# Layer B's q as seven products for eight, with weight operands made in layer A and kept in DRAM

## The chip, the cores and the metric

The kernel runs on one core of one Trainium2 chip. The metric is the time of the kernel on the device in microseconds (us). Before the change the median of three runs is 1050.8 us (1050.23 to 1050.91).

## The reference

The input x is 1024 tokens by 1024 channels in float32. Layer A is a gated MLP on chunks of 128 tokens, layer B is sliding-window attention. Cut to what matters:

```python
# layer A
h = rms_norm(x, a_pre_g)
u, v, z = split(h @ w_in, 3)                 # each 1024 x 2048
v = layer_norm(gelu(v), ln_g, ln_b)          # then in 8 groups of 256 channels
s = causal(w_s[group]) @ v[chunk] + b_s
h = x + rms_norm((gelu(u) * s * silu(z)) @ w_out, a_post_g)
# layer B
k = rms_norm(h, kv_norm_g) @ w_k             # 1024 x 256, 4 heads of 64
v = rms_norm(h, kv_norm_g) @ w_v
q, z = split(rms_norm(h, b_pre_g) @ b_w_in, 2)   # each 1024 x 1024, 16 heads of 64
logits = q k^T / 8 + alibi                   # window of 128 back, with a sink per head
o = softmax(logits with sink) @ v
out = h + rms_norm((o * silu(z)) @ b_w_out, b_post_g)
```

## The kernel before

Each float32 product is made from two float32r parts. A value is split into a high part (a copy on ScalarE) and a low part (the rest, a subtraction on DVE), and `mm3` (L168 to L171) issues three matmuls: high times high, high times low, low times high. One matmul has 128 rows, 128 columns of weights and mostly 512 columns of tokens, half of the sequence. The halves are called h = 0 and 1.

In layer A the three big products (`v_layer`, `uz_layer`, `out_layer`) use a scheme of seven products of half-size matrices instead of eight: the two token halves and the two halves of the inner dimension give sums and differences of the inputs, and the same is done with the weights, on DVE, GpSimd and ScalarE. In layer B all products are plain.

Layer B runs in this order. `q_phase(0)` makes q for the first half (192 matmuls of 512 columns), while `chain_a(1)` finishes layer A's output h1 for the second half beside it. `kv_phase(0)` makes k and v (48 matmuls of 512 columns and 96 of 256). `z_phase(0)` makes the gate z (192). Then `attn(0)` runs the attention of the first half. Attention's matmuls come in small groups with softmax work on DVE, ScalarE and GpSimd between them, so `attn` fills the gaps from a generator: `more` takes a share of 64 fill steps at each of 40 places. The fill of `attn(0)` is `kv_phase(1)`, `q_phase(1)` and the first half of `z_phase(1)`. `attn(1)` is filled with the second half of z and with the output product `out_b`.

The weights of layer B go through the class `Weights` (L112 on). `order` lists the pieces of 512 KB in the order of their use, `load` fetches a raw piece on the queue of SyncE (SP), and `split` makes whi (ScalarE, L109) and wlo (DVE, L110), scaled by the gain of the norm. Three raw buffers and two buffers each of whi and wlo take turns. A weight that is used by both halves is fetched and split twice.

The order of the instructions on each engine is set by a scheduler that goes by the program's order, dependencies and its own estimates. It may move an instruction ahead of another, except where `keep_in_program_order` pins it. Each engine then works through its list in that order, and an instruction that waits holds all behind it. Loads and stores are issued on the queue of SP; a few stores are issued on the queue of ScalarE (ACT); GpSimd (POOL) issues none. A tile whose tag has fewer buffers than tiles waits until the last reader of the old content is done.

At the start of the program GpSimd has a cast, two selects (`affine_select`, L593) that cut the causal triangle of the weights w_s, and then `rx`, the factors of the first norm, for which ScalarE's gelu waits.

## Time and profile before

| what | number |
|---|---|
| median of three runs | 1050.8 us |
| profiled execution | 1051.19 us |
| its span | 1049.4 us |
| TensorE (PE) busy | 1038.2 us, 99% |
| VectorE (DVE) busy | 731.8 us, 70% |
| ScalarE (ACT) busy | 579.8 us, 55% |
| GpSimd (POOL) busy | 199.5 us, 19% |
| granted TensorE clock, mean | 0.998 |
| moved by DMA | 157.56 MB, 150 GB/s over the span |

The span goes from the first to the last instruction of the trace, and the profiled execution's own time is 1.8 us longer. A share of busy time is an average over the span: stages of the program differ, and what a wait costs is read at its own place. "A <- B" in a list of waits says that A stood still until B's result was there.

### The profile page before, as it was taken

Reading aid. Unit: us, or ns where it says so; the run is one execution under the profiler, and the core shown is the slowest. Engines: PE = TensorE matmul, PEld = TensorE weight load, DVE = VectorE, ACT = ScalarE, POOL = GpSimd, SP = SyncE. Lnnn points to the kernel's source line nnn. Section 1 sums busy time; section 2 is a strip of 40 time slices with the busy share of each in tenths; the row PEclk is TensorE's granted clock in tenths of the full one; section 3 lists DMA queues with packets and bytes.
Section 4 is the critical chain, followed back from the end, with each engine's and each line's share of the span. In section 5 each row is a group of like instructions: output and inputs, shape, how many; then the busy total and the mean of one; then the engine's idle time right before and its main releaser. Section 6 shows DMA issues by size and latency. Waiting matters only on the chain.

```text
span 1049.4 us, 13678 instructions
## 1 busy us (share of the span) xinstructions
PE 1038.2 (99%) x4994; PEld 854.8 (81%) x4994; DVE 731.8 (70%) x1244; ACT 579.8 (55%) x998; POOL 199.5 (19%) x153
## 2 busy tenths in 40 slices
PE   9999999999999999999999999999999999999997
PEld 7878888888888888888888888888888777877776
DVE  6987566867768668677696587765247786667763
ACT  6584344565565465655444465654466665786631
POOL 0500003253442552530200000100001111011120
PEclk9999999999999999999999999999999999999999
DMA  8878242324333333247998543532322121211363
GB/s 309 271 262 292 101 171 94 116 101 146 126 117 120 123 134 116 101 140 265 320 354 282 195 167 93 200 102 82 99 81 66 56 81 61 81 61 62 121 220 121
DMA packets 80899, 157.56 MB, mean 150 GB/s; under 512 B 5824, under 2 KB 32704, under 8 KB 80832
## 3 DMA queue, kind: packets, MB, share of 16 engines
q1 hardware_dynamic: 76320, 148.01, 41.4%
q10 hardware_dynamic: 4512, 8.68, 2.3%
q8 instruction: 39, 0.64, 0.3%
q14 instruction: 28, 0.23, 0.1%
HBM read 125.21 MB, written 31.46 MB: 149 GB/s over the span
## 4 chain that ended last, share of the span: by engine, by line
PE 93%; DVE 3%; DMA 2%; ACT 1%; issue 0%; SPq 0%; DVEq 0%; POOLq 0%; ACTq 0%
PE qz L169 6%; PE ob L169 6%; PE ub L169 6%; PE qz L171 6%; PE ub L170 6%; PE ub L171 6%; PE ob L171 6%; PE ob L170 6%; PE qz L170 6%; PE s L1058 3%; PE uc L170 3%; PE uc L169 3%; PE uc L171 3%; PE sp L621 3%; PE oc L169 2%; PE oc L171 2%
## 5 line engine op out<-in xcount | busy, mean ns | idle before, releaser
L110 DVE SCALAR_TENSOR_TENSOR wlo<-raw_w,gn,whi 128x512 fp32r<-128x512 f32 x80 | 58.5, 757 | 62.2 <-ACT whi L109 62.0
L169 PE MATMUL qz<-n_hi,whi 128*128 128x512 f32 x256 | 100.9, 394 | 0.0
L171 PE MATMUL qz<-n_hi,wlo 128*128 128x512 f32 x256 | 99.8, 390 | 1.1 <-DVE wlo L110 1.1
L170 PE MATMUL qz<-n_lo,whi 128*128 128x512 f32 x256 | 99.9, 390 | 0.0
L109 ACT ACTIVATE whi<-raw_w,gn 128x512 fp32r<-128x512 f32 x80 | 54.8, 716 | 56.8 <-PE qz L170 36.6
L1073 ACT ACTIVATE pr<-pr,mx 128x129 f32<-128x129 f32 x128 | 50.1, 393 | 39.8 <-DVE mx L1069 39.8
L169 PEld LDWEIGHTS qz<-n_hi,whi 128*128 128x128 f32 x256 | 48.1, 188 | 15.8 <-issue 5.7
L105 ACT ACTIVATE uzhilo_g<-f 128x1024 fp32r<-128x1024 f32 x31 | 32.9, 1060 | 49.2 <-PE uc L171 43.3
L171 PEld LDWEIGHTS qz<-n_hi,wlo 128*128 128x128 f32 x256 | 48.0, 188 | 11.8 <-DVE wlo L110 1.5
L170 PEld LDWEIGHTS qz<-n_lo,whi 128*128 128x128 f32 x256 | 48.1, 188 | 9.3
L106 DVE TENSOR_TENSOR uzhilo_g<-f,uzhilo_g 128x1024 fp32r<-128x1024 f32 x31 | 38.6, 1245 | 19.9 <-ACT uzhilo_g L105 19.9
L209 ACT ACTIVATE uz_slots<-ub 128x512 f32<-128x512 f32 x48 | 28.3, 590 | 42.4 <-PE ub L171 39.2
L169 PE MATMUL ub<-T,whi_g 128*128 128x512 f32 x128 | 50.7, 396 | 0.0
L169 PE MATMUL ub<-T,uzhilo_g 128*128 128x512 f32 x128 | 50.5, 395 | 0.0
L171 PE MATMUL ub<-T,wlo_g 128*128 128x512 f32 x128 | 49.9, 390 | 0.0
L171 PE MATMUL ub<-T,uzhilo_g 128*128 128x512 f32 x128 | 49.9, 390 | 0.0
L170 PE MATMUL ub<-T,uzhilo_g 128*128 128x512 f32 x128 | 49.9, 390 | 0.0
L170 PE MATMUL ub<-T,whi_g 128*128 128x512 f32 x128 | 49.8, 389 | 0.0
L169 PE MATMUL uc<-T,uzhilo_g 128*128 128x512 f32 x124 | 48.9, 395 | 0.0
L170 PE MATMUL uc<-T,uzhilo_g 128*128 128x512 f32 x124 | 48.3, 389 | 0.0
L171 PE MATMUL uc<-T,uzhilo_g 128*128 128x512 f32 x124 | 48.3, 389 | 0.0
L105 ACT ACTIVATE whi_g<-raw_uz 128x1024 fp32r<-128x1024 f32 (+1 forms) x31 | 26.5, 854 | 36.8 <-PE ua L170 14.3
(334 smaller groups left out, 3078.3 us busy)
## 6 DMA issues: line engine op xcount, KB each, us to landing
raw_uz<-in_wuz_in_dram SPq DMA_DIRECT2D x32, 512.0 KB, 3.4
raw_w<-in_wqz_dram SPq DMA_DIRECT2D x32, 512.0 KB, 3.5
td<-uz_slots SPq DMA_DIRECT2D x56, 256.0 KB, 2.2
orawP2a<-td SPq DMA_DIRECT2D x28, 512.0 KB, 4.1
raw<-in_wv_in_dram SPq DMA_DIRECT2D x17, 512.0 KB, 4.8
vg<-vd SPq DMA_DIRECT2D x8, 1024.0 KB, 5.3
orawP2b<-in_wo_a_dram SPq DMA_DIRECT2D x16, 512.0 KB, 8.2
vraw<-in_wv_in_dram SPq DMA_DIRECT2D x13, 512.0 KB, 4.8
```

The costliest lines, as they stand in the source:

```text
L105: nc.scalar.activation(hi, src, AF.Copy)
L106: nc.vector.tensor_tensor(lo, src, hi.bitcast(F32), ALU.subtract)
L109: nc.scalar.activation(hi, src, AF.Copy, scale=g)
L110: nc.vector.scalar_tensor_tensor(lo, src, g, hi.bitcast(F32), ALU.mult, ALU.subtract)
L169: nc.tensor.matmul(out, lhsT=a_hi, rhs=b_hi, start=start, stop=False, skip_group_check=True)
L170: nc.tensor.matmul(out, lhsT=a_hi, rhs=b_lo, start=False, stop=False, skip_group_check=True)
L171: nc.tensor.matmul(out, lhsT=a_lo, rhs=b_hi, start=False, stop=stop, skip_group_check=True)
L209: nc.scalar.activation(out, a, AF.Copy)
L621: nc.tensor.matmul(psv[:, n], lhsT=d["vg"][:, 4 * j + n, i * P:(i + 1) * P], rhs=d["wc"], start=True, stop=True)
L1058: nc.tensor.matmul(pss[par][:, g, w0:256], lhsT=q[par][:, m, bs_], rhs=w[par][:, p, ks], start=g + k == 0, stop=g + k == 2, skip_group_che ...
L1073: nc.scalar.activation(pr[:, i], pr[:, i], AF.Exp, bias=mx[:, i:i + 1], scale=-1.0, accum_out=dn[:, i:i + 1])
```

## The change

q of both halves becomes seven products for eight. The operands on the side of the tokens are made from n0 and n1, the normed inputs of both halves, in `norm_sums`: T1 and T2 are the two inner halves of n0, T3 is one of n1, and T4 to T7 are sums, split anew. The operands on the side of the weights are made in layer A: `q_pieces` fetches the raw q weights in 16 pieces, scales them on GpSimd (two operations of 128x2x128), forms the sums on DVE (four operations of 128x128, and two subtractions for the low parts), copies the high parts on ScalarE, and stores high and low parts in the DRAM tiles `qw`. Fourteen pieces are made inside `uz_layer` and two inside `out_layer`. `QTiles` reads them back in 16 loads of a pair each, on GpSimd's queue, through a ring of four buffers, two of which are the whi and wlo buffers of the weights.

The split weights of twelve pieces (z's and kv's for the first use) are stored in DRAM (`keep`, on SP's queue), and their second use is a load of the stored pair on GpSimd's queue in place of a fetch and a split.

Layer B's order is new: the first half of z and all of kv for h = 0, with `chain_a(1)` and `norm_sums` beside them; their results go to DRAM (`zd`, `kd`). Then the early products of q (T1 and T2, 96 matmuls) and the late ones (T6, T5, T7, T3, T4 for each of four output pairs, 240 matmuls), whose results go to DRAM (`qd`) and are read back and split by `reload_q`. Eight steps of `kv_phase(1)` come before `attn(0)`, and its fill of 40 steps is the rest of it, the second half of z for h = 0 and the first half for h = 1. The q of h = 1 is reloaded beside it.

In layer A, a small select on GpSimd stands ahead of the causal ones, one group of gelus is put off, and some gelu, silu and normalising operations are pinned in program order.

```diff
     class Weights:
-            self.order += q + kv + z + kv + q + z
+            self.order += z[0:4] + kv + kv + z[4:8] + z
+            self.kept = {n: dram.tile([2, P, 1024], F32, name=f"ws{n}") for n in (*range(8), *range(12, 16))}
+            self.again = dict(zip((*range(8, 12), *range(16, 24)), (*range(4, 8), *range(4), *range(12, 16))))
...
+        def keep(self, n):
+            if n in self.kept:
+                for w, part in zip(self.kept[n], self.done[n]):
+                    nc.sync.dma_start(out=w, in_=part.bitcast(F32))
         def split(self, i):
...
+                if n != 8:
+                    self.keep(n - 1)
+                if n in self.again:
+                    for w, part in zip(self.kept[self.again[n]], (hi, lo)):
+                        nc.gpsimd.dma_start(out=part, in_=w.bitcast(F32R))
...
+    def q_pieces(first, last, s, lo, hi_tile):
+        def put(q, k, hi, j0, n):
+            for hl, t in enumerate((hi, lo)):
+                nc.sync.dma_start(out=qw[q][hl][:, k, j0:j0 + n], in_=t[:, 0:n].bitcast(F32))
...
+        for n in range(first, last):
+            q, k = divmod(n, HT)
+            for i in range(2):
+                v = s[:, 0:4].rearrange("p (m l) c -> p l m c", l=2)[:, i]
+                pin(nc.gpsimd.tensor_scalar(v, v, gain(G_BPRE, i * HT + k), None, ALU.mult))
+            yield
+            pin(add(s[:, 4], s[:, 2], s[:, 3], ALU.add))
+            pin(add(s[:, 5], s[:, 4], s[:, 0], ALU.subtract))
+            pin(add(s[:, 2], s[:, 0], s[:, 2], ALU.subtract))
+            pin(add(s[:, 6], s[:, 1], s[:, 5], ALU.subtract))
+            for j0, w in ((0, 4), (4, 3)):
+                hi = hi_tile(f"qhi{n}_{j0}")
+                pin(copy(hi[:, 0:w], s[:, j0:j0 + w]))
+                yield
+                pin(add(lo[:, 0:w], s[:, j0:j0 + w], hi[:, 0:w].bitcast(F32), ALU.subtract))
+                put(q, k, hi, j0, w)
...
+        nc.gpsimd.tensor_copy(mv[:, 0], p0[0][:, 1022:1024].bitcast(F32))
+        nc.gpsimd.affine_select(mv[:, 0], mv[:, 0], [[1, 2]], ALU.is_ge, 0.0, base=0, channel_multiplier=0)
...
+    class QTiles:
+        def __init__(self):
+            w = pair_of(wpool, "w", 2)
+            self.ring = Ring(self.half(1), w, w, self.half(0))
+            self.pieces = [(q, (0, 1)) for q in range(4)]
+            self.pieces += [(q, j) for q in range(4) for j in ((4, 5), (6,), (2, 3))]
...
+        def load(self):
...
+            for t, src in zip(v, qw[q]):
+                nc.gpsimd.dma_start(out=t, in_=src[:, :, js[0]:js[0] + n].bitcast(F32R))
...
+        def early_products(self):
+            for q in range(4):
...
+                self.product(q, 1, b, True, False)
+                copy(self.p1[q], b)
+                yield
+                self.product(q, 2, b, False)
+                copy(c, b)
...
+        def late_products(self, rest):
+            for q in range(4):
...
+                self.product(q, 6, b, True, False)
+                add(c01, p1, b, ALU.add)
...
+                self.product(q, 5, cc, True, False)
...
+                self.product(q, 7, b, False, False)
+                add(c11, p1, b, ALU.add)
...
+                self.product(q, 3, cc, False)
...
+                self.product(q, 4, b, False)
+                add(c10, p1, b, ALU.add)
...
-    fill = chain(kv_phase(1, n1), q_phase(1, n1, q1), z_phase(1, n1, z1, 0, 4))
-    attn(0, q0, z0, fill, 64)
+    fill = chain(kv_phase(1, n1), z_phase(0, n0, z0, 4, 8), z_phase(1, n1, z1, 0, 4))
+    attn(0, q0, z0, fill, 40, first=8, side=side)
```

The start of GpSimd's list before the change (`wc` is the causal weights, `rx` the factors of the norm):

```order
L422 CAST whi_v0_140<-raw_v0_133 128x512 x2
L593 ISA
L593 AFFINE_SELECT wc0_1226<-wc0_1226 128x128
L593 AFFINE_SELECT wc1_1342<-wc1_1342 128x128
L179 TENSOR_TENSOR rx0_87<-rx0_87,small_85 128x4
```

and with the change:

```order
L486 CAST whi_v0_160<-raw_v0_153 128x512 x2
L492 COPY mv_103<-whi_v0_160 128x2
L493 ISA
L493 AFFINE_SELECT mv_103<-mv_103 128x2
L658 AFFINE_SELECT wc0_1248<-wc0_1248 128x128
L658 AFFINE_SELECT wc1_1366<-wc1_1366 128x128
L200 TENSOR_TENSOR rx0_99<-rx0_99,small_85 128x4
```

A small select, and the row that comes with the first select, have moved ahead of the causal ones.

The loads and stores of SP in the first phase of layer B before the change (`raw_w` are raw weights, `xa` tokens, `h1d` layer A's output, `gpb` a gain):

```order
L101 DMA raw_w_4987<-in_wqz_dram 128x4x256
L745 DMA xa_1_5024<-in_x_dram 128x1024
L101 DMA raw_w_5036<-in_wqz_dram 128x4x256
L736 DMA gpb<-in_b_post_dram 128x1024
L761 DMA h1d_0_76<-yoa_2_4284 128x1024
L761 DMA h1d_1_77<-yoa_2_4284 128x1024
L745 DMA xa_2_5044<-in_x_dram 128x1024
L745 DMA xa_3_5056<-in_x_dram 128x1024
L101 DMA raw_w_5082<-in_wqz_dram 128x4x256
```

and with the change (`ws` are the kept split weights):

```order
L106 DMA raw_w_5178<-in_wqz_dram 128x4x256
L261 DMA q_slots<-in_x_dram 128x1024 x3
L828 DMA xa_3_5276<-in_x_dram 128x1024
L144 DMA ws_87<-whi_5282 128x1024
L144 DMA ws_87<-wlo_5283 128x1024
L106 DMA raw_w_5296<-in_wqz_dram 128x4x256
L144 DMA ws_88<-whi_5288 128x1024
L144 DMA ws_88<-wlo_5289 128x1024
L106 DMA raw_w_5351<-in_wkv_dram 128x1024
L844 DMA h1d_0_76<-yoa_2_4590 128x1024
```

The token loads (`q_slots` is used for three of them) have moved together ahead of it, and two stores of split weights stand behind each raw weight.

TensorE at the end of the last late q and the first kv matmuls of h = 1 (`p13` and `p15` are pieces of q's weights, `p13` with T6 and T5 in the buffer that `whi8` takes next, `pk` the sums of k); this passage is new, and before it kv of h = 1 began inside `attn(0)`:

```order
L192 MATMUL qc3_6156<-qT5_5379,wlo_p13_6075 128x512
L190 MATMUL qb3_6155<-qT7_0_5893,qhilo0_p15_6138 128x512
...
L192 MATMUL qb3_6155<-qT7_0_5893,qhilo0_p15_6138 128x512
L190 MATMUL pk1_0_6286<-n1_hi_5269,whi8_6186 128x512
L191 MATMUL pk1_0_6286<-n1_lo_5270,whi8_6186 128x512
L190 MATMUL pk1_1_6287<-n1_hi_5269,whi8_6186 128x512
L191 MATMUL pk1_1_6287<-n1_lo_5270,whi8_6186 128x512
L190 MATMUL qb3_6155<-qT4_0_5381,qhilo0_p15_6138 128x512
```

Twelve matmuls lie between the last reader of p13 and the first of whi8, and four of kv's matmuls have moved between T7 and T4 of q.

350 lines of the change are left out of this document (273 added, 77 removed).

## The prediction

> **What bounds the kernel now.** I read the first part of the page (busy time of each engine) and the fourth (the chain that ended last) first, because they say which engine a saving has to be taken from.
>
> ```profile
> span 1049.4 us, 13678 instructions
> PE 1038.2 (99%) x4994; PEld 854.8 (81%) x4994; DVE 731.8 (70%) x1244; ACT 579.8 (55%) x998; POOL 199.5 (19%) x153
> ...
> PE 93%; DVE 3%; DMA 2%; ACT 1%; issue 0%; SPq 0%; DVEq 0%; POOLq 0%; ACTq 0%
> ```
>
> TensorE is busy for 99% of the span and carries 93% of the chain. The profiled execution took 1051.2 us, 1.8 us more than its span and 0.4 us above the median of the three runs (1050.8). The sum below is made against 1051.2, and 0.4 us is taken off at its end. Next the waits of TensorE over the whole span (what waited, on which producer; us in total, times, longest), and beside them the one wait of ScalarE that stands behind the first row.
>
> ```profile
> PE vb L169 <- ACT ve L209: 1.3, 1, 1.3
> PE warm L931 <- DVE small L93: 1.1, 1, 1.1
> PE qz L171 <- DVE wlo L110: 1.1, 1, 1.1
> ...
> ACT vslot L391 <- POOL rx L179: 2.1, 1, 2.1
> ```
>
> Only two waits of any size lie inside the program (the warm matmul is its start). So a matmul taken out is worth its full time, as long as the new order leaves no new wait. What one matmul is worth is read from the timeline of TensorE in layer B's q; columns are start, duration, engine, line.
>
> ```profile
> 654.60 0.39 PE L169 MATMUL qz<-n_hi,whi 128*128 128x512 f32 x1
> ...
> 681.80 0.39 PE L169 MATMUL qz<-n_hi,whi 128*128 128x512 f32 x1
> ```
>
> Between these two rows lie 120 matmuls: 27.20/120 = 0.2267 us each. The 0.39 us is its stay in the pipeline; 0.39 - 0.23 = 0.16 us is what a consumer waits after the last one.
>
> **The matmuls removed.** q takes 2 x 192 = 384 matmuls of 512 columns before. Seven products of 4 k-tiles x 3 for each of 4 output pairs are 7 x 48 = 336. All other groups stay in number. 48 x 0.2267 = **10.9 us less**.
>
> **The warm-up on GpSimd.** Its first rows in the timeline:
>
> ```profile
> 39.02 13.03 POOL L593 TENSOR_SCALAR_AFFINE_SELECT wc<-wc 128x128 f32<-128x128 f32 x2 [30.87 <-DMA wc<-in_ws_t_dram]
> 52.03 1.01 POOL L179 TENSOR_TENSOR rx<-rx,small 128x4 f32<-128x4 f32 x1
> ```
>
> Two selects of one shape take 13.0 us together while rx stands behind them in the queue; ScalarE's gelu waits for rx, and TensorE for the bank that ScalarE frees. The change runs a small select some 20 us earlier, where GpSimd was idle for 30.9 us. If the first call is what was long, the 1.3 us wait goes. Bounds 0 and 1.3; I take **1.3 less**.
>
> **The wait of 1.1 us in q** stands where the raw weights and an x tile shared one queue. In the change x's tiles are fetched ahead of z, so I take **1.1 less**, between 0 and 1.1. That leaves 1051.2 - 10.9 - 1.3 - 1.1 = 1037.9.
>
> **What is added on TensorE's path.** These rows give durations (busy sum, mean ns; then idle before).
>
> ```profile
> L209 ACT ACTIVATE ve<-vb 128x512 f32<-128x512 f32 x8 | 4.8, 596 | 3.0 <-PE vb L171 2.6
> L105 ACT ACTIVATE n_hi<-nt 128x512 fp32r<-128x512 f32 x16 | 8.7, 586 | 2.0 <-PE nt L776 2.0
> L106 DVE TENSOR_TENSOR n_lo<-nt,n_hi 128x512 fp32r<-128x512 f32 x16 | 10.3, 682 | 0.7 <-ACT n_hi L105 0.7
> L206 DVE TENSOR_TENSOR uz_slots<-ub,bc 128x512 f32<-128x512 f32 x16 | 11.0, 688 | 20.7 <-PE ub L171 20.7
> ```
>
> (1) Early products: the second product goes on in the bank of the first, so it waits for ScalarE's copy, 0.16 + 0.60 = 0.76 us and the semaphores, and only one to four matmuls or a few transposes stand between. Bounds 0 and 1.0 each; I take 0.45, four times, 1.8. (2) The first late product T6 needs the last sums: from the last transposes n_hi 0.59, three DVE operations of 0.68 and T6's own split 0.59 + 0.68 make 3.9 us with little between them, against 12 matmuls (2.7 us) and the head of the next product that cover it. Bounds 0 and 1.2; I take 0.65. (3) In each late q, T4 goes on in T7's bank after DVE has read it (0.16 + 0.69 and the semaphores), behind 4 bridging matmuls of 0.91: 0.1 each, 0.4 in all. Sum **2.9**.
>
> **The read-backs.** Before, no load stands on GpSimd's queue, so the trace has no duration for them. The nearest rows of the DMA issues (KB each, us to landing):
>
> ```profile
> raw_w<-in_wqz_dram SPq DMA_DIRECT2D x32, 512.0 KB, 3.5
> td<-uz_slots SPq DMA_DIRECT2D x56, 256.0 KB, 2.2
> ...
> vg<-vd SPq DMA_DIRECT2D x8, 1024.0 KB, 5.3
> orawP2b<-in_wo_a_dram SPq DMA_DIRECT2D x16, 512.0 KB, 8.2
> ...
> tmp_o<-in_wo_a_dram SPq DMA_DIRECT2D x6, 512.0 KB, 8.7
> ```
>
> A pair (high and low part, 512 KB each) lands in 5.3 us if it goes as one load of 1 MB; by the slope from 256 to 512 KB, 3.5 + 2 x 1.3 = 6.1 us; 8.2 to 8.7 where the queues are full. Against it stands the time from the last matmul on the buffer's old content to the first on the new, counted in matmuls on TensorE's order: 28 matmuls, 6.35 us, for the pair with T7 and T4 in the second, third and fourth late q; 7.3 to 8.2 us for the pair with T6 and T5; 6.4 us to 10 us for the split weights inside first attention. The worst place is the first kv weight, whi8: it takes the buffer of T6 and T5 of the last q, and the scheduler has put four kv matmuls only 12 matmuls, 2.7 us, behind them. Its high part alone needs 3.5, with its low part 5.3: 0.8 to 2.6 us, up to 6 with full queues. I take 1.5 there, and 0.3 for each of the three pairs with 6.35: **2.4**.
>
> **DMA and DVE.** Rows of the windows (us, then busy time and count of PE, PEld, DVE, ACT, POOL, then clock, DMA share and GB/s):
>
> ```profile
> 654.60:699.50 44.90, 43.85 (x193) 35.93 (x192) 28.29 (x41) 24.82 (x42) 3.82 (x3) 1.00 0.48 166
> 698.15:720.60 22.45, 22.45 (x151) 20.57 (x150) 15.53 (x23) 11.79 (x20) 0.00 (x0) 1.00 0.27 82
> 525.00:550.00 25.00, 25.00 (x112) 20.72 (x111) 23.75 (x25) 12.83 (x18) 0.00 (x0) 1.00 0.98 355
> 769.00:894.20 125.20, 125.20 (x681) 99.93 (x680) 90.76 (x254) 82.04 (x215) 15.32 (x14) 1.00 0.22 68
> ```
>
> z's first half and kv now last 21.8 + 22.4 = 44 us. In them go eight weight pairs out (8.4 MB), some 3.1 MB of pieces in, 2.1 MB of raw weights, 1 MB each of h1 and z: about 15.6 MB, 350 GB/s, as much as the full row (355 at share 0.98), where this stage had 166. Raw weights are asked for some 11 us ahead, more than 8.7; the first pieces have 9. Bounds 0 and 6; I take 0.6. The 2.4 MB that two pieces add to the full row itself delay loads that TensorE did not wait for there: bounds 0 and 4, I take 0. In the layer before, six small DVE and two ScalarE operations and two on GpSimd per piece run where DVE was 70% busy: 0.
>
> First attention was 125.2 us. Out go q1's 192 matmuls (43.5) and half of kv (11.2); z's second half comes in (21.8): 92.3 us. DVE's 90.8 us in it change by these rows:
>
> ```profile
> L110 DVE SCALAR_TENSOR_TENSOR wlo<-raw_w,gn,whi 128x512 fp32r<-128x512 f32 x32 | 23.8, 772 | 13.9 <-ACT whi L109 13.9
> ...
> L980 DVE SCALAR_TENSOR_TENSOR q_lo<-qz,qsc,q_lo 64x512 fp32r<-64x512 f32 x8 | 6.0, 755 | 0.1
> L980 DVE SCALAR_TENSOR_TENSOR q_hi<-qz,qsc,q_hi 64x512 fp32r<-64x512 f32 x8 | 6.0, 744 | 1.7 <-ACT q_lo L976 1.5
> ```
>
> Three quarters of the splits go (23.8 x 3/4 = 17.9) and q's 12.0; twelve operations of 64x1024 come, by the nearest row 1.28 us each:
>
> ```profile
> L760 DVE SCALAR_TENSOR_TENSOR yoa<-yoa,rpa,xa 128x1024 f32<-128x1024 f32 x4 | 5.0, 1283 | 2.2 <-POOL rpa L179 1.2 <-DMA xa<-in_x_dram 0.9
> ```
>
> 90.8 - 17.9 - 12.0 + 15.4 = 76.3 us, 0.83 of the stage instead of 0.73. Bounds 0 and 12.3 (below, third rival); I take **0.3**. GpSimd's selects stand behind read-backs that wait for a weight buffer; a select is needed some 8 us after its scores, so this is in the same bound.
>
> **The sum:** 1037.9 + 2.9 + 2.4 + 0.6 + 0.3 = 1044.1; 0.4 less, as the median stands below the profiled run: 1043.7.
>
> [...] The trace of before has DVE 0.70 busy, with fp32 subtractions of 128x512 in 0.68 us, and shows no load of GpSimd's queue beside them. [...]
>
> **Rivals.** *Read-backs too slow* (slower than before). Landing at L, a pair costs L less its slack wherever L is above it; a weight that comes late gives the next one that much more time, so about every second pays. At 8.2 us: three pairs x 1.85, whi8 5.5, and four weights 0.8 to 1.7 give 16; at 8.7 about 20. Instead of 2.4 this makes 1057 to 1061. It decides from about 7.3 us on, where the costs reach the 10 us that are won. For it speaks that no GpSimd load was seen and that 512 KB did take 8.2 us; against it that this was at 355 GB/s, and the late products need about 3.2 MB in 13.6 us, 240 GB/s. *All is covered:* the copies and read-backs just fit; only half of the 2.9 is paid: 1037.9 + 1.4 - 0.4 = 1039. For it speaks that TensorE waited 3.5 us in all before. *First attention becomes DVE's:* if DVE can't be filled above its old share there, 90.8/125.2 = 0.725, the stage takes 76.3/0.725 = 105 us, 12.7 more, 1056; at 0.77 it is 99 us, 1050. Against it speaks 23.75 of 25 us in the full row above; for it that the chain from scores to weights of a head goes through DVE twice and that 12 fill matmuls instead of 18 stand between them.
>
> **How the numbers follow.** Forecast (1040.5 to 1047.5): 0.48. All covered (1037 to 1040.5): 0.15. Read-backs too slow (1049 to 1066): 0.21. Attention bound (1046 to 1056): 0.12. Anything else, such as a saturated DMA stage, 0.04. The likeliest time is **1043.7**. The range is **1038 to 1057**: it leaves out the upper half of the slow read-backs and a little at the bottom. 0.2% is 2.1 us, about what a measurement of this kernel can tell from no change, so faster means below 1048.7. Faster: 0.48 + 0.15 + 0.01 + 0.05 + 0.01 = 0.70. Same (to 1052.9): 0.03 + 0.05 + 0.01 = 0.09. Slower: 0.17 + 0.02 + 0.02 = 0.21.
>
> **What would show it.** TensorE should have 48 rows fewer and no wait on ve at 52 us; its waits should name qa on ScalarE, qb on DVE, and pk of half 1 on a load into whi8 of 1 to 3 us. If the median landing of the pieces on GpSimd's queue is above 7.3 us, or waits on such loads sum to over 5 us, the first rival holds. If TensorE waits in first attention for DVE's maxima or sums, and DVE's share there stays near 0.73, the third does. The prediction is wrong at its root if matmuls in the shorter q are further apart than 0.2267 us with no wait named.

## The result and the profile after

The changed kernel takes 1073.8 us (median of four runs, 1070.78 to 1077.11); the kernel before, run beside it, 1050.9. The ratio is 1.0222, with a 95% interval of 1.021 to 1.0235: 2.2% slower. The forecast was 1043.7, in a range of 1038 to 1057. The profiled execution of the changed kernel took 1070.8 us, the fastest of its runs. First, from its page, the size of the program, each engine's busy time and the chain that ended last:

```profile
span 1069.1 us, 14044 instructions
PE 1036.3 (97%) x4946; PEld 844.3 (79%) x4946; DVE 795.6 (74%) x1330; ACT 541.2 (51%) x962; POOL 273.0 (26%) x243
...
PE 65%; DVE 14%; DMA 7%; issue 6%; ACT 4%; POOL 3%; SPq 0%; DVEq 0%; POOLq 0%; ACTq 0%
```

There are 48 matmul rows fewer, as forecast, but TensorE's share of the chain fell from 93% to 65%. 14% now stands with DVE and 7% with DMA. The waits of TensorE over the whole span (us in total, times, longest):

```profile
PE ub L190 <- ACT uz_slots L233: 11.2, 6, 1.9
PE qb L192 <- DMA wlo_p<-qw: 3.5, 3, 1.7
PE qb L192 <- DMA qhilo_p<-qw: 3.3, 2, 1.8
PE o L1364 <- POOL pc L1350: 1.6, 2, 1.2
PE pk L192 <- DMA wlo<-ws: 1.2, 1, 1.2
...
PE o L1364 <- DVE mx L1328: 1.0, 1, 1.0
```

The largest wait is in layer A, in `uz_layer`, which the forecast gave a cost of 0. For a table by stage, each stage runs from its first matmul to the first matmul of the next. "Without losses" is the stage of before, less or plus the matmuls that left or came at 0.2267 us each and kv's half (11.2) and z's half (21.8) that moved.

| stage (us) | before | without losses | after |
|---|---|---|---|
| v of layer A | 157.0 | 157.0 | 156.7 |
| u and z of layer A | 335.8 | 335.8 | 350.2 |
| output product of layer A | 155.9 | 155.9 | 156.7 |
| z, q and kv, up to the first scores | 114.4 | 136.5 | 146.1 |
| attention to the end | 273.6 | 240.6 | 247.4 |
| sum | 1036.7 | 1025.8 | 1057.1 |

The second column holds the 10.9 us of removed matmuls by its making (1036.7 - 1025.8). That they were won is borne out by the 48 rows that are gone and by the spacing of the rest: where nothing waits, the late products still stand 0.2267 us apart (19 of them between 789.65 and 793.96). Against them 31.3 us were lost: 14.4 in u and z, 9.6 in z, q and kv, 6.8 in attention, 0.5 in the rest. Two windows show the stage of u and z; columns are us, then busy time and count of PE, PEld, DVE, ACT and POOL, then clock, DMA share, GB/s. Before:

```profile
162.90:498.70 335.80, 335.80 (x1618) 282.55 (x1617) 245.75 (x362) 183.81 (x224) 124.86 (x93) 1.00 0.39 132
```

After, with two later stretches (the late products of q with kv's first steps, and most of first attention):

```profile
162.50:512.70 350.20, 338.98 (x1618) 283.23 (x1617) 305.42 (x446) 162.16 (x225) 156.67 (x121) 1.00 0.51 174
...
740.90:815.50 74.60, 67.87 (x312) 54.72 (x313) 24.63 (x33) 9.67 (x12) 20.09 (x26) 1.00 0.88 242
815.50:905.00 89.50, 85.53 (x477) 65.36 (x476) 70.42 (x222) 67.08 (x186) 21.32 (x22) 1.00 0.49 166
```

In u and z the same 1618 matmuls take 14.4 us longer. DVE has 84 operations more and 59.7 us more of busy time, but it is busy for 0.87 of the stage and so, as a sum, not its bound. What stops TensorE is one place that comes six times. The timeline around the first of the six (start, duration, engine, line; in brackets the idle time before and what ended it):

```profile
213.11 1.67 POOL L227 TENSOR_TENSOR f<-raw_uz,raw_uz 128x512 f32<-128x512 f32 x1 [7.21 <-DVE uzhilo_g L111]
213.55 5.35 DVE L679 TENSOR_SCALAR vg<-vg,mv,ve 128x256 f32<-128x256 f32 x4
214.74 1.34 POOL L227 TENSOR_TENSOR f<-raw_uz,f 128x512 f32<-128x512 f32 x1
...
218.82 3.06 DVE L227 TENSOR_TENSOR qs<-qs 128x128 f32<-128x128 f32 x4
220.68 0.39 PE L192 MATMUL ub<-T,wlo_g 128*128 128x512 f32 x1
221.77 0.63 ACT L233 ACTIVATE qhi<-qs 128x512 fp32r<-128x512 f32 x1 [4.96 <-DVE qs L227]
222.31 1.07 ACT L233 ACTIVATE uz_slots<-ub 128x512 f32<-128x512 f32 x2
222.94 0.50 PE L190 MATMUL ub<-T,whi_g 128*128 128x512 f32 x1 [1.87 <-ACT uz_slots L233]
```

Read it from the bottom. TensorE waits for ScalarE to empty the bank `ub`. ScalarE's copy stands behind `qhi<-qs`, the high part of a piece of q's weights, and that has waited 4.96 us for DVE's four sums `qs`. These stand behind the normalising operations of `vg`. Both rows of DVE are long: four `vg` take 5.35 us, while GpSimd runs sums beside them. In before, seven of the same operations, with no sum on GpSimd beside them, took 2.35 us:

```profile
244.20 2.35 DVE L614 TENSOR_SCALAR vg<-vg,mv,ve 128x256 f32<-128x256 f32 x7 [0.34 <-DMA vg<-vd]
```

The next TensorE product in this stage thus hangs on a chain over three engines, because of where one copy stands in ScalarE's list. All six stalls show the same rows, with the same 4.96 us on ScalarE. The 1.87 us is counted from the modelled end of the last matmul; with the 0.16 us between its hand-over and that end, TensorE starts 2.03 us late. The last two groups to compare are the DMA issues of the read-backs (KB each, us to landing) and the timeline of one of them:

```profile
qhilo_p<-qw POOLq DMA_DIRECT2D x12, 512.0 KB, 6.9
...
wlo_p<-qw POOLq DMA_DIRECT2D x6, 512.0 KB, 7.4
```

```profile
770.39 1.48 POOL L1135 DMA_DIRECT2D qhilo_p<-qw  x2 [8.14 <-PE qc L192]
778.64 0.50 PE L192 MATMUL qb<-qT,qhilo_p 128*128 128x512 f32 x1 [1.75 <-DMA qhilo_p<-qw]
```

This is the pair with T7 and T4 of the third late q. GpSimd takes 0.74 us to issue each of its two loads, so the low part starts 0.74 us late; with a landing of 6.9 to 7.4 us it is there 7.6 to 8.1 us after the buffer is free. The forecast had a slack of 6.35 there; the difference, 1.3 to 1.8, fits the wait shown (1.75). All five waits are on low parts. Three are on the pairs with T7 and T4 of the second, third and fourth late q (1.1, 1.8 and 1.5 us), two on the pairs with T6 and T5 of the third and fourth (0.6 and 1.7), for which the forecast saw 7.3 to 8.2 us of slack and put nothing.

The weight whi8, at which the forecast saw the worst place, was not waited for. Its first matmul, and the wait on split weights that is in the list above:

```profile
798.50 0.39 PE L190 MATMUL pk<-n_hi,whi 128*128 128x512 f32 x1
...
818.98 0.50 PE L192 MATMUL pk<-n_hi,wlo 128*128 128x512 f32 x1 [1.22 <-DMA wlo<-ws]
```

The matmuls at 798.50 follow the one before at 0.23 us. The 1.22 us, and 0.15 us just before it on the high part, belong to the third weight of kv, after the first scores.

### The profile page after: what moved, and what is told of

Read it like the earlier page. It is cut to its first block, busy times and chain, and to the rows that moved or that the text cites. A ratio compares the mean times of both kernels' runs of the same rounds, so it can differ in the third digit from the quotient of the medians.

```text
span 1069.1 us, 14044 instructions
## 1 busy us (share of the span) xinstructions
PE 1036.3 (97%) x4946; PEld 844.3 (79%) x4946; DVE 795.6 (74%) x1330; ACT 541.2 (51%) x962; POOL 273.0 (26%) x243
## 4 chain that ended last, share of the span: by engine, by line
PE 65%; DVE 14%; DMA 7%; issue 6%; ACT 4%; POOL 3%; SPq 0%; DVEq 0%; POOLq 0%; ACTq 0%
PE ob L190 5%; PE ob L191 4%; PE ob L192 4%; DVE vg L679 4%; PE ub L190 4%; PE ub L191 3%; PE ub L192 3%; PE sp L686 2%; DVE uz_slots L227 2%; PE s L1317 2%; PE z L190 2%; PE z L192 2%; PE z L191 2%; DMA wlo_p<-qw 2%; DVE qs L227 2%
## 5 line engine op out<-in xcount | busy, mean ns | idle before, releaser
L190 PE MATMUL ub<-T,whi_g 128*128 128x512 f32 x128 | 52.2, 408 | 11.2 <-ACT uz_slots L233 11.2
L227 POOL TENSOR_TENSOR f<-raw_uz 128x512 f32<-128x512 f32 x15 | 22.9, 1526 | 125.4 <-DMA raw_uz<-in_wuz_in_dram 100.4
L190 PE MATMUL z<-n_hi,whi 128*128 128x512 f32 x128 | 50.9, 397 | 0.0
L191 PE MATMUL ub<-T,whi_g 128*128 128x512 f32 x128 | 50.6, 395 | 0.0
L192 PE MATMUL z<-n_hi,wlo 128*128 128x512 f32 x128 | 50.1, 393 | 0.1
L191 PE MATMUL z<-n_lo,whi 128*128 128x512 f32 x128 | 50.2, 392 | 0.0
L679 DVE TENSOR_SCALAR vg<-vg,mv,ve 128x256 f32<-128x256 f32 x64 | 47.5, 794 | 0.0
L227 POOL TENSOR_TENSOR f<-raw_uz,raw_uz 128x512 f32<-128x512 f32 x15 | 21.8, 1452 | 96.9 <-DVE uzhilo_g L111 96.9
L233 ACT ACTIVATE qhi<-qs 128x512 fp32r<-128x512 f32 (+1 forms) x28 | 16.1, 574 | 54.7 <-DVE qs L227 45.6
L1349 POOL TENSOR_SCALAR_AFFINE_SELECT pp<-pc 128x1024 f32<-128x1024 f32 x14 | 18.0, 1288 | 93.4 <-ACT pc L1346 93.4
```

Of the source, the lines that this page charges most:

```text
L190: nc.tensor.matmul(out, lhsT=a_hi, rhs=b_hi, start=start, stop=False, skip_group_check=True)
L191: nc.tensor.matmul(out, lhsT=a_hi, rhs=b_lo, start=False, stop=False, skip_group_check=True)
L192: nc.tensor.matmul(out, lhsT=a_lo, rhs=b_hi, start=False, stop=stop, skip_group_check=True)
L227: return (eng or nc.vector).tensor_tensor(out, a, b, op)
L233: return nc.scalar.activation(out, a, AF.Copy)
L679: pin(nc.vector.tensor_scalar(vg[:, n], vg[:, n], mv[:, n, 0:1], ve[:, n:n + 1], ALU.subtract, ALU.mult))
```

## The experiments

Every ratio is against the kernel before, run beside it on the same chip; the edits stand against the changed kernel, but for those that say otherwise. The theories at the start: the loss in u and z comes from the q pieces, either because DVE and GpSimd slow each other where they run together, or because the work sits in the wrong place of the in-order lists; the loss in q comes from landing times.

**Normalising not pinned.**

```diff
-                pin(nc.vector.tensor_scalar(vg[:, n], vg[:, n], mv[:, n, 0:1], ve[:, n:n + 1], ALU.subtract, ALU.mult))
+                nc.vector.tensor_scalar(vg[:, n], vg[:, n], mv[:, n, 0:1], ve[:, n:n + 1], ALU.subtract, ALU.mult)
```

> The change with one edit: the normalising operations of layer A's v (64 on DVE, 128x256) are no longer pinned in program order. The instructions of TensorE, GpSimd and SyncE keep their order; on DVE half of each group moves ahead of the split before it, out of the time in which GpSimd forms sums. Theory A: the six waits of 1.9 us for uz_slots (11.2 us) come from the place of these operations: beside GpSimd's sums they take 1.38 us instead of 0.41, and the sums for q's weights and the copy on ScalarE come late behind them. Then their mean falls from 794 to below 500 ns, the wait for uz_slots from 11.2 to below 2 us, the stage from 350 to 337 to 340 us, and the time from 1073.8 to 1060 to 1064. Rival B: the added work for q's weights is too much for the stage wherever the normalising stands: the wait stays above 6 us and the time above 1068.

Measured: 1088.3 us, ratio 1.0367 (1.034 to 1.0395). The group of `vg` (busy sum, mean ns, idle before):

```profile
L679 DVE TENSOR_SCALAR vg<-vg,mv,ve 128x256 f32<-128x256 f32 x64 | 25.0, 451 | 4.7 <-DMA vg<-vd 3.3 <-POOL ve L576 1.2
```

and two of the waits, TensorE's and ScalarE's largest in this stage:

```profile
PE ub L190 <- ACT uz_slots L233: 16.5, 11, 3.2
...
ACT uz_slots L695 <- DVE uz_slots L227: 79.3, 22, 6.4
```

The mean of `vg` fell from 794 to 451 ns, so the slowing beside GpSimd is gone, and yet u and z took 359.7 us, 9.5 more. Rival B's signs came (a wait above 6 us, a time above 1068), but neither theory had the stage slower. The waits of TensorE are not the same ones. In the changed kernel:

```profile
L190 PE MATMUL ub<-T,whi_g 128*128 128x512 f32 x128 | 52.2, 408 | 11.2 <-ACT uz_slots L233 11.2
```

and here:

```profile
L190 PE MATMUL ub<-T,uzhilo_g 128*128 128x512 f32 x128 | 53.0, 414 | 16.6 <-ACT uz_slots L233 16.5
```

The six stalls before the products with `whi_g` are gone, and eleven others stand before those with `uzhilo_g`. A likely reason is in the waits above: ScalarE's silu (L695) now waits 79.3 us for DVE, against 24.2 in the changed kernel, and holds the copies behind it. The edit changed the length and the place of `vg` at once, so this run can't tell one from the other.

**The late read-backs on SyncE's queue.** The question is whether GpSimd's queue, with 0.74 us of GpSimd's time to issue each load, makes the landing of 6.9 to 7.4 us.

```diff
-                nc.gpsimd.dma_start(out=t, in_=src[:, :, js[0]:js[0] + n].bitcast(F32R))
+                nc.sync.dma_start(out=t.bitcast(F32), in_=src[:, :, js[0]:js[0] + n])
```

> The change with one edit: the 16 read-backs of q's weight pieces (32 loads) are issued on SyncE's queue in place of GpSimd's. [...] Rival B: it is the traffic of that stage or the runs of 1 KB: the landing stays above 6.3 us, the waits above 4 us and the time above 1071.

**The same loads on GpSimd's queue, from a DRAM layout in which each is one run of 4 KB (2 KB for a single piece) per partition.**

```diff
-    qw = [[dram.tile([P, HT, 7, P], F32, name=f"qw{q}{i}") for i in range(2)] for q in range(4)]
+    qw = [[dram.tile([P, HT * 7 * P], F32, name=f"qw{q}{i}") for i in range(2)] for q in range(4)]
...
-                nc.gpsimd.dma_start(out=t, in_=src[:, :, js[0]:js[0] + n].bitcast(F32R))
+                nc.gpsimd.dma_start(out=t[:, 0:n * 512], in_=src[:, js[0] * 512:(js[0] + n) * 512].bitcast(F32R))
```

> The change with one edit: q's weight pieces lie in DRAM so that each read-back reads one run of 4 KB (or 2 KB) per partition instead of four of 1 KB (or 512 B); they stay on GpSimd's queue, and the stores are cut into more and shorter runs (three for two). Theory B (the runs of 1 KB make the read-backs slow): landing falls from 6.9 to 7.4 us to 4 to 5.5 us, near the 3.6 and 4.9 of the split weights on the same queue; TensorE's waits for these loads fall from 6.8 to below 2 us; time 1066 to 1069. Theory A (the queue or the traffic): landing stays above 6.3 us and the time above 1071.

**Both together.**

> The change with both edits of the read-backs of q's weights: on SyncE's queue and in runs of 4 or 2 KB. If queue and runs each add to the landing (6.9 to 7.4 us; 5.6 to 6.0 with SyncE alone, 5.7 to 5.9 with long runs alone), it falls to 4.5 us or less, no wait for these loads is left, the late stage is 66 to 68 us, and the time 1067 to 1070. If it is the traffic of the stage, the landing stays at 5.5 and the time is within 1.5 us of 1069.3, that of SyncE alone.

Measured: 1069.3 us (ratio 1.018, 1.0164 to 1.0195), 1072.5 (1.0217, 1.0202 to 1.0233) and 1068.9 (1.0179, 1.0164 to 1.0195). The late stage took 70.9, 69.6 and 69.9 us instead of 74.7. The DMA issues with SyncE's queue:

```profile
wlo_p<-qw SPq DMA_DIRECT2D x6, 512.0 KB, 6.0
```

On GpSimd's with the long runs:

```profile
qhilo_p<-qw POOLq DMA_DIRECT2D x12, 512.0 KB, 5.8
```

Either edit brings the landing under the slack of 6.35 and takes nearly all of the waits for q's pieces (6.8 us before the edits; 0.7 left by the first and 1.0 by the second). The two hardly add (5.0 to 5.6 together). So neither the queue alone nor the length of the runs explains the landing; that what is left comes from the traffic of this stage, a DMA share of 0.88, is likely and not shown. Part of the gain moves on: the waits for kv's split weights, 1.4 us in the changed kernel, are 2.9, 2.0 and 3.5 us in these runs, and whi8 is now waited for, with 0.6 to 1.2 us. The stage is 4 to 5 us shorter, of the 31.3 us lost. The second edit's time hardly moved all the same; in its profiled execution v, and u and z, each took 1.6 us more than in the changed kernel's.

**The small select alone, in the kernel before.**

```diff
+        nc.gpsimd.tensor_copy(mv[:, 0], p0[0][:, 1022:1024].bitcast(F32))
+        nc.gpsimd.affine_select(mv[:, 0], mv[:, 0], [[1, 2]], ALU.is_ge, 0.0, base=0, channel_multiplier=0)
```

> The kernel before with the change's small select on GpSimd alone added at the same place. Theory: the first select's long first call moves into GpSimd's idle time, rx is there some 10 us earlier, the wait of 1.3 us in the v product is gone and the time falls by 1.3 us to 1049.5 (0.12%). Rival: the next producer is as late, the wait stays or moves, and the time is the same within 0.3 us.

Measured: 1050.8 us against 1050.8, ratio 1.0002 (0.9993 to 1.001). GpSimd's timeline:

```profile
9.16 0.19 POOL L428 TENSOR_SCALAR_AFFINE_SELECT mv<-mv 128x2 f32<-128x2 f32 x1
39.44 12.70 POOL L595 TENSOR_SCALAR_AFFINE_SELECT wc<-wc 128x128 f32<-128x128 f32 x2 [30.09 <-DMA wc<-in_ws_t_dram]
```

and the wait of TensorE that was to go:

```profile
PE vb L169 <- ACT ve L209: 1.3, 1, 1.3
```

The two causal selects still take 12.70 us (13.03 without it), and the wait is the same 1.3 us. Alone in the kernel before, the early select is worth nothing. Why the causal ones are long stays open. In the profiled execution of the changed kernel the wait at this place is not there: its first causal select took 7.71 us and its second 0.70. In the eight other runs that keep the change's v product the wait is 2.3 us, and v takes 158.3 to 160.2 us for 156.7.

**No arithmetic on q's weights inside u and z.** The scaling, the sums and the splits of the fourteen pieces are left out there, so that the values of q are not those of the reference; the loads, the stores and everything else stay.

```diff
-                pin(nc.gpsimd.tensor_scalar(v, v, gain(G_BPRE, i * HT + k), None, ALU.mult))
-            pin(add(s[:, 4], s[:, 2], s[:, 3], ALU.add))
...
-                pin(copy(hi[:, 0:w], s[:, j0:j0 + w]))
-                pin(add(lo[:, 0:w], s[:, j0:j0 + w], hi[:, 0:w].bitcast(F32), ALU.subtract))
```

> The change with the arithmetic on q's weights left out in the stage of u and z (the 14 pieces there: no scaling on GpSimd, no sums and low parts on DVE, no copies on ScalarE; the raw weights are stored in their place, so q is made from wrong operands; the loads, the stores and all pins of other operations stay, and TensorE's instructions are the same). Theory A, the work: with DVE back from 0.87 to about 0.73 of that stage the waits for uz_slots fall from 11.2 to below 1 us, the stage from 350 to 336 to 338, the time from 1073.8 to 1058 to 1061. Rival B, the pins: gelu, silu and normalising in program order alone hold the copies up, the waits stay above 5 us, the time above 1066.

**No pins at all in the pieces, the normalising, the silus and the gelus.**

```diff
-                pin(copy(hi[:, 0:w], s[:, j0:j0 + w]))
+                copy(hi[:, 0:w], s[:, j0:j0 + w])
...
-            if g + 1 < G:
-                pin(silu)
```

> The change with no operation of the stage of u and z pinned in program order (normalising, silu, gelu and all of q's weight work are free for the scheduler); all work stays. Theory A, the work: DVE stays near 0.87, so the waits only move: they stay above 6 us and the time above 1067, as with the normalising alone unpinned (1088). Rival B, the pins: waits below 3 us and 1059 to 1063.

Measured: 1066.7 us (ratio 1.0152, 1.0137 to 1.0167) and 1098.7 (1.0459, 1.0441 to 1.0476). The window of u and z without the arithmetic:

```profile
164.20:506.00 341.80, 337.61 (x1618) 283.70 (x1617) 269.92 (x362) 150.20 (x198) 127.78 (x93) 1.00 0.54 177
```

and TensorE's wait:

```profile
PE ub L190 <- ACT uz_slots L233: 4.2, 1, 4.2
```

The six stalls are gone. One of 4.2 us at another place stays, with 1.7 us lost at half clock behind it (the last section has the clock): 5.9 us, about all that this stage has above the 335.8 of before. There DVE waits 4.67 us for the load of `vg` from DRAM (at 301.68), ScalarE's silu waits for DVE, and the copy for TensorE stands behind it. `vg` is still slow here (796 ns mean), so an operation that is slow beside GpSimd is not enough for the six stalls; the added work is needed. Without pins u and z took 376.0 us and the wait on `ub` 25.5 us: the pins are a help, not the cause.

**Twelve weights split again instead of read back.**

```diff
-            self.kept = {n: dram.tile([2, P, 1024], F32, name=f"ws{n}") for n in (*range(8), *range(12, 16))}
-            self.again = dict(zip((*range(8, 12), *range(16, 24)), (*range(4, 8), *range(4), *range(12, 16))))
+            self.kept = {}
+            self.again = {}
```

> The change without keeping split weights: none is stored, and the second use is a fetch of the raw weight on SyncE's queue and a split, as before the change. Theory A: the stores of 12.6 MB and the read-backs on GpSimd's queue cost more than the splits: the stage of z and kv falls from 46.2 to 44.5 to 45.2 us, the waits for whi and wlo (1.4 us) and for GpSimd's selects (1.6 us) go, the time falls to 1069 to 1071. Rival B: DVE, with 18 us more in first attention, becomes late there: the attention is 3 us longer or more and the time above 1075.

Measured: 1081.2 us, ratio 1.0292 (1.0275 to 1.0309). The part from first attention on took 252.0 us instead of 247.4, with a wait of 2.8 us of z's matmuls on ScalarE's split. z and kv took the same 46.2 us without the stores of the split weights: the traffic of the kept weights costs nothing there, and keeping them pays in attention.

**The sums of a piece ahead of the normalising.** The theory by now: what counts is what ScalarE's copy of a piece has to wait for. If DVE makes the four sums before the `vg` operations, the copy comes early, and `ub` is freed in time.

```diff
             else:
+                step(pieces_q)
                 normalise(g)
-            step(pieces_q)
+            if zz:
+                step(pieces_q)
```

> The change with one step moved: in the quads where v is normalised, the four sums for q's weights (DVE) stand ahead of the eight normalising operations in place of behind them. TensorE, GpSimd and SyncE keep their order; ScalarE's copies keep their order but for one split. Theory: the 2.0 us stalls come from ScalarE's queue, in which the copy of q's sums waits for DVE and stands ahead of the two copies that free TensorE's bank; with the sums made first the copy is not late, the six waits (11.2 us) go, the stage falls from 350 to 337 to 341 us and the time from 1073.8 to 1060 to 1064. Rival: DVE as a whole is late there, the normalising operations (seven of them beside GpSimd's sums now) hold up the split that follows, and the wait for uz_slots or for that split stays above 6 us, the time above 1068.

Measured: 1068.1 us, ratio 1.0162 (1.0144 to 1.0181). u and z took 341.3 us instead of 350.2. The same group as above:

```profile
L679 DVE TENSOR_SCALAR vg<-vg,mv,ve 128x256 f32<-128x256 f32 x64 | 59.1, 982 | 0.0
```

and the waits, one of them new:

```profile
PE ub L190 <- ACT uz_slots L233: 3.3, 5, 1.0
PE ob L192 <- DVE ohiloP0a L111: 2.8, 1, 2.8
```

`vg` became slower still (982 ns), and the wait fell from 11.2 to 3.3 us. Where it stands:

```profile
L190 PE MATMUL ub<-T,uzhilo_g 128*128 128x512 f32 x128 | 50.7, 396 | 3.3 <-ACT uz_slots L233 3.3
```

All six stalls before the products with `whi_g` are gone, and five shorter waits stand at the other place. With `vg` slow and the sums early there is no stall of the first kind, so its cause is that the sums stand behind the slow `vg`. The wait of 2.8 us in the output product may be an effect of this edit: runs that leave this order alone show 0 to 1.6 us there, the five with the sums first and `vg` pinned 1.3 to 3.0.

**The order of v as before, and no early select.**

```diff
-        nc.gpsimd.tensor_copy(mv[:, 0], p0[0][:, 1022:1024].bitcast(F32))
-        nc.gpsimd.affine_select(mv[:, 0], mv[:, 0], [[1, 2]], ALU.is_ge, 0.0, base=0, channel_multiplier=0)
...
-            late = ({(7, 0): (a1, 0), (3, 0): (e67, 1)}, {(5, 0): (a1, 0)})[Q].get((m, u))
+            late = {(7, 0): (a1, 0), (3, 0): (e67, 1)}.get((m, u)) if Q == 0 else None
...
```

> The change with its part in the v product undone: no small select at the start, no gelus put off or pinned; all else stays. Theory: the stall at 53 us is 1.3 us again, as in the kernel before, in place of 2.3 us with a half-speed stretch of TensorE's clock behind it, and the v stage is 157 us in place of 158.3 to 160.2; the time falls by 1.5 to 3 us to 1071 to 1072.3. Rival: the stall depends on the first selects alone and the time is the same within 1 us.

**Three edits together: the sums first, the order of v, the late read-backs on SyncE's queue.**

> The change with three edits at once: the sums ahead of the normalising, the v product as before, and the read-backs of q's weights on SyncE's queue. If each gives what it should alone (11 to 13, 1.5 to 3 and 4.5 us), the time is 1054 to 1057, still above the 1050.8 of the kernel before, with 7 us lost in attention and 5 in the late products and first kv; if the sums' place does not help, it is 1066 to 1068.

Measured: 1072.7 us in the first run (ratio 1.0207, 1.0191 to 1.0223), which cannot be told from the changed kernel, although the stall in v was 1.3 instead of the 2.3 us of most runs. The three together give 1061.1 (1.0106, 1.0079 to 1.0133): 12.7 us less than the change, the best of all versions, 4 us more than expected, and still 1% slower than before. What is left of the waits:

```profile
PE ub L190 <- ACT uz_slots L233: 4.4, 7, 1.0
PE pk L192 <- DMA wlo<-ws: 2.7, 2, 1.4
```

Its u and z took 343.2 us, the late part 71.0, attention to the end 246.9, all at full clock. The next four runs start from this version and change one thing each.

**The read-backs of the split weights on SyncE's queue too.**

```diff
-                        nc.gpsimd.dma_start(out=part, in_=w.bitcast(F32R))
+                        nc.sync.dma_start(out=part.bitcast(F32), in_=w)
```

> The three edits of the run before (1061.1) and a fourth: the 24 read-backs of split weights go on SyncE's queue too, so that no load stands on GpSimd's queue and its selects in attention wait for none. If the queue is what costs in first attention and the first kv (waits for whi and wlo 3.1 us, for GpSimd's select 1.6 us), the waits fall to below 1.5 us in all and the time to 1057 to 1059. If those loads are late because their buffer comes free late, and the selects because ScalarE and DVE hand on late, the time stays within 1 us of 1061.

Measured: 1068.5 us, ratio 1.017 (1.0148 to 1.0191), 7.4 us more. SyncE's own queue has a likely reason:

```profile
SPq L158 <- PE z L192: 52.4, 8, 9.8
```

A read-back waits up to 9.8 us for its buffer, and the loads and stores behind it wait with it. Attention to the end took 256.6 us for 246.9, with new waits of TensorE at the first scores (3.0 us on the split of k, 1.7 on a maximum) and 10.2 us at half clock behind the first of them. The output product took 5.0 us more too, with 6.8 us at half clock, and there this edit changes no load, so not all of the 7.4 us is shown to be its doing.

**The normalising not pinned, with the sums first.** The edit is that of the first experiment, on this version.

> The three edits of the run at 1061.1 (sums first, v as before, q's read-backs on SyncE's queue) with the normalising no longer pinned as a fourth. Open is whether the 5 to 7 us that the stage of u and z is still longer than before come from normalising beside GpSimd's sums (0.98 us each there) or from DVE's amount of work. If the first: the mean falls to 0.45, the stage to 336 to 338 and the time to 1055 to 1057. If the second, as when the normalising alone was unpinned: the waits for uz_slots go up above 8 us and the time above 1068.

Measured: 1084.0 us, ratio 1.0313 (1.0298 to 1.0328), with u and z at 365.6:

```profile
PE ub L190 <- ACT uz_slots L233: 20.8, 10, 4.4
...
ACT uz_slots L694 <- DVE uz_slots L227: 85.6, 22, 6.6
```

`vg` is at 452 ns and DVE busy for 276.6 us only, against 305.4, and the stage is the second slowest of all. So neither faster normalising nor less busy time on DVE helps by itself. As in the first experiment it is the silus that wait for DVE; that they hold the copies up is likely and not shown by a run of its own.

**q's reloads for h = 1 out of first attention; and six steps of kv before it instead of eight.**

```diff
-    side = chain(iter(range(1)), reloads(0, 2, 3), iter(range(2)), reloads(1, 0, 1, 2, 3))
+    side = chain(iter(range(1)), reloads(0, 2, 3))
...
-    attn(0, q0, z0, fill, 40, first=8, side=side)
+    attn(0, q0, z0, fill, 42, first=6, side=side)
```

The first edit belongs to the first run, with the reloads run after first attention; the second to the second run.

> The three edits of the run at 1061.1, and the eight operations each of ScalarE and DVE that read q of the second half back (four of six pieces) are moved out of first attention to the gap ahead of second attention. Theory: those operations, 1.15 and 1.28 us each, stand ahead of attention's maxima and copies and make them late; then the waits for the select, the maxima and the rest in first attention fall from 3.6 us to about 1, while at the start of second attention TensorE waits some us for q. Rival: with 12 fill matmuls for 18 attention is late without them too, and the waits in first attention stay above 3 us.

> The three edits of the run at 1061.1, with six steps of kv ahead of first attention in place of eight and 42 in its fill in place of 40. If the thin fill is what makes attention late, its waits fall by half a us or more and the time by 0.5 to 2 us; if not, the time is the same within 1 us.

Measured: 1062.2 us (ratio 1.0111, 1.0096 to 1.0127) and 1063.9 (1.0129, 1.0112 to 1.0146). Attention to the end was 248.0 in the first. In the second it was 250.2, with 68.8 for the late part: 319.0 in sum, against 317.9. In neither did it come nearer to the 240.6 without losses. The named waits there are 1.4 us on split weights, 1.6 on a select, 1.0 on a maximum and 0.6 on a sum in the changed kernel; the other 2.2 of the 6.8 us have no name, and neither the reloads nor the thin fill is shown as their cause.

## Why the prediction was wrong

**The step that failed** is "In the layer before, six small DVE and two ScalarE operations and two on GpSimd per piece run where DVE was 70% busy: 0." I asked only whether DVE had room, and it had (0.70 is the share of the whole span; in this stage it was 0.73). The cost came by way of order. ScalarE's pinned copy of a piece waits for DVE's sums, the sums stand behind the normalising, and behind ScalarE's copy stand the copies that empty `ub` for TensorE. The term measured 14.4 us: six stalls of 2.03 us (12.2, of which 11.2 are named waits), 1.7 us of half clock, and 0.5. The runs that show it: taking the arithmetic out removes the six stalls, and so does making the sums ahead of the normalising, though `vg` stays slow in both. They give 8.4 and 8.9 of the 14.4 us back; what is left in them are waits at another place.

That the operations are slower beside GpSimd than their nearest rows (25.5 us more for `vg` alone, 47.5 against 22.0) was missed too, and the stalls seem to need it as well as the order. An estimate from the timeline of the first stall: four `vg` at 0.41 us each would end the chain 3.7 us earlier, more than the wait of 1.87. The unpinned run agrees as far as it goes: with `vg` fast these six stalls are gone, but others come, since it moved `vg` as well.

**The read-backs** were mis-sized, at 2.4 us. The three pairs at 0.3 each measured 4.4 us, and the pairs with T6 and T5, at nothing, 2.4. I took a landing of 5.3 to 6.1 from loads in stages of 0.22 to 0.48 DMA share; it was 6.9 to 7.4 in one of 0.88, and GpSimd's 0.74 us of issue for each half of a pair was not in the sum at all. The traffic was as expected (242 GB/s for 240), but 242 GB/s kept the DMA engines busy for 0.88 of the stage here. whi8's 1.5 measured 0, by luck: the wait of 1.5 us on the pair before it, at 796.09, gave its load that much more time, and where the pairs come sooner, whi8 is waited for with 0.4 to 1.2 us. Its low part, which the forecast added, is not needed before 805.01. The waits of 1.4 us on a split weight are those of the third one, which the forecast put at nothing. This is the rival "read-backs too slow" by its signs, waits of 8.2 us in sum where it set 5, at half its price. It alone would have left the kernel at about 1050.

**The rest, by terms.** Removed matmuls: 10.9, as put. The wait of 1.1 in q went, as put. Early products, T6 and T7 to T4 (2.9) and the traffic of z and kv (0.6): z, q and kv lost 9.6 + 1.1 - 6.8 = 3.9 us beside the late loads, against 3.5 in sum; T4's wait, put at 0.4, shows no wait. The warm-up, 1.3, is 0 by the run of the small select alone: the bound of 0 was the right one. That the profiled execution has no wait on `ve` at 52 us, as forecast, has to be called luck: eight other runs with the same v product wait 2.3 us there. First attention at 0.3: attention to the end lost 5.4 beside the third weight of kv, within the term's bounds of 0 to 12.3 (12.7 by the third rival's own working). DVE was busy for 0.79 of most of first attention, under the 0.83 that it should have reached; the third rival's waits on maxima and sums are there, with 1.6 us.

By stages against the forecast's own sum (1044.1 for the profiled run): v 1.0, u and z 14.4, the output product 0.8, z, q and kv 4.8, attention 6.5 more, and 0.8 less at the edges of the program: 26.7, which is 1070.8. The median lies 3.0 us above that execution, not 0.4 below, and the kernel's runs now spread over 6.3 us. One likely reason is the wait of 2.3 us in v that this execution was spared; the last section has another.

## What to carry to other kernels

An operation that is added to an engine with room costs what it holds up, not what it takes. Follow it through its engine's list and ask whether anything behind it frees a bank or a buffer that TensorE is about to need, and what it waits for itself; here a copy of 0.63 us cost TensorE 2 us, six times. A load's cover has to be counted from the moment the buffer is free, with the issue time of each part in it, at the DMA share that the stage will have after the change: here 0.74 us a part, and 6.9 to 7.4 us to landing at a share of 0.88.

## What was not expected of the hardware

**The clock.** A stall of 2.03 us cost 3.7 here. The two windows around a stall in u and z of the changed kernel:

```profile
307.90:311.30 3.40, 1.53 (x8) 0.95 (x6) 3.40 (x5) 1.23 (x3) 1.94 (x2) 1.00 0.60 225
311.40:314.80 3.40, 3.40 (x9) 2.63 (x10) 2.90 (x4) 0.80 (x2) 3.27 (x2) 0.50 0.64 213
```

and TensorE's timeline there:

```profile
308.98 0.39 PE L192 MATMUL ub<-T,wlo_g 128*128 128x512 f32 x1
311.24 0.70 PE L190 MATMUL ub<-T,whi_g 128*128 128x512 f32 x1 [1.87 <-ACT uz_slots L233]
311.74 0.63 PE L191 MATMUL ub<-T,whi_g 128*128 128x512 f32 x1
312.17 0.63 PE L192 MATMUL ub<-T,wlo_g 128*128 128x512 f32 x1
```

After the stall the matmuls stand 0.43 us apart, not 0.23, at a granted clock of 0.50, for 3.4 us: 1.7 us lost on top. In the traces of all 17 kernels, wherever the clock changes more than once, the changes lie on a grid of 3.413 us: in the changed kernel's, half speed lasts from 311.361 to 314.774, and the next change comes 750.93 us later, 220 steps of the grid. For each window of that grid at full clock I summed TensorE's idle time, from the hand-over of one matmul to the start of the next. All 28 windows with 2.03 us or more were followed by one at half speed, and so were two of the three between 2.02 and 2.03. Of some 3480 windows with less, four were (1.5 to 1.9 us); what sets these apart is open. The six stalls of the changed kernel are 2.03 us long. In the profiled execution one lies in a single window of the grid and was followed by half speed; the other five lie across two windows each, with at most 1.95 us in one, and were not. By these counts, where the stalls fall on the grid would decide how many of them cost 1.7 us more. That would give much of the spread of its runs (mean clocks of 0.993 to 0.998 in the four), but the cause of the spread is argued, not shown.

**DVE beside GpSimd.** The group of the normalising operations in the kernel before:

```profile
L614 DVE TENSOR_SCALAR vg<-vg,mv,ve 128x256 f32<-128x256 f32 x64 | 22.0, 407 | 4.7 <-DMA vg<-vd 3.5 <-POOL ve L511 1.2
```

In the changed kernel:

```profile
L679 DVE TENSOR_SCALAR vg<-vg,mv,ve 128x256 f32<-128x256 f32 x64 | 47.5, 794 | 0.0
L227 DVE TENSOR_TENSOR qs<-qs 128x128 f32<-128x128 f32 x56 | 26.1, 505 | 14.2 <-POOL qs L333 13.7
```

Single operations of `vg` go from 0.41 us alone to 1.38 to 1.45 (25 of the 64), beside GpSimd sums of 1.29 to 1.67, and those of `qs` from 0.28 to 1.26 or more (12 of the 56), beside sums of 1.32 to 1.42. The long durations come out near those of the sums; what makes DVE take longer is not shown. Of the read-backs of 512 KB, those that GpSimd issues landed in 6.9 to 7.4 us and SyncE's in 5.6 to 6.0; with the long runs in 5.7 to 5.9 and in 5.0 to 5.6.
